# Order of the quarter blocks of two chained MLP products, of their operands and of the last gate mixes, in a one-core decoder layer

## The chip, the cores and the metric

One NeuronCore of one Trainium2 chip runs the whole layer as one program. The metric is device time in microseconds, the median of repeated executions. The kernel before takes 1119.97 us (three runs, 1119.68 to 1120.58).

The core has a matrix engine (TensorE, PE in the profile; its weight loads are PEld), VectorE (DVE), ScalarE (ACT), GpSimd (POOL) and SyncE (SP). In this kernel SP issues the plain loads and POOL issues the DMAs that add what they fetch onto what already lies in SBUF.

## What is computed

One decoder layer on 512 tokens of 1024 features, fp32. Behind the two attention-like branches stand the gated sum, an output projection, and a squared-ReLU MLP of 4096 hidden features:

```python
mixed = jax.nn.sigmoid(gr) * a_ret + jax.nn.sigmoid(gm) * a_mla
x = x + mixed @ w_o

h2 = rms_norm(x, norm_mlp)
x = x + jnp.square(jax.nn.relu(h2 @ w_up)) @ w_down

gate = jax.nn.sigmoid(rms_norm(x, norm_ple) @ w_ple_gate)
x = x + gate * (p_l @ w_ple)
```

The two MLP products and the output projection are what the change touches.

## The kernel before

**Three matmuls for one.** Every fp32 operand is split in two parts that TensorE takes at its fast fp32 rate: ScalarE rounds it (names with h: `wh_`, `ch`, `xu..h`), VectorE subtracts the rounded part from the original (names with l: `wl_`, `cl`, `xu..l`). `mm3` then issues low times high, high times low and high times high. So each weight chunk of 128x1024 costs one ScalarE instruction (line 262) and one VectorE subtraction (line 266) before the matrix engine can use it, in `load_chunk`.

**Seven products for eight.** From the second of four groups on (`gg` = 0 to 3, 1024 hidden features each) the up product (`up_seven`, names `us`, weights `..up<gg><p><c>`) and in all four groups the down product (`down`, names `dn`, weights `..dn<gg><p><c>`) run in seven quarter blocks instead of eight, numbered p = 1 to 7. A block takes its weights in two chunks, c = 0 and 1, of 512 KB. The weights of blocks 1, 2 and 3 are loaded as they are (tiles `wr_`). Block 7 needs a sum of two quarters of the matrix, block 6 that sum with a third quarter added, block 4 with a fourth. These three share one place in SBUF (tile `dr_..7`): a load, an addition by DMA for 7, another for 6 once 7's low part has been taken, another for 4 once 6's has. Block 5 is a sum of two in its own tile. `prepare` (lines 215 to 246) issues the loads on SP (line 234) and the additions on POOL (line 224).

**Operands.** `combine` makes the down product's seven operands from the hidden activations `f` (sums `s`, `s1`, then `xsplit` into `ch`, `cl`). The up product's seven operands `xu1` to `xu7` are made once, in the first group, by `up_operand`, from the normalised input `x2n`, and serve the groups 1 to 3. `down_out` adds a block's result to the output tiles `d` (line 1105).

**What sets the order.** `step` collects the work as a list, and `run_steps` walks it: weights are split one chunk ahead and prepared three chunks ahead. The framework then places each engine's instructions by its own planning, except that matmuls stay in program order. Three buffers each hold the high and the low parts (`NW`), six the raw chunks of blocks 1, 2, 3 and 5 (`NRAW`), four the running sums (`NDRAW`). A high part of a chunk can be written only when TensorE is done with the chunk three before it. Four PSUM tiles of two banks serve the MLP.

Ahead of the MLP, the last part of a branch (`branch_r`, weights `br`) alternates with the gate mixes (`mix`, lines 908 to 912), then come the first halves of two output columns (`out_part`, four of the eight `mixed` operands each), then the rest of the projection (`out_proj`).

The order of the blocks in groups 0 to 2 is one line; a name with u is a block of the next group's up product, a bare number a block of this group's down product:

```python
order = [1, 7, 2, 6, 5, 4, 3]
seq = [1, 7, 2, 6, "u1", 5, "u7", 4, "u6", 3, "u2", "u5", "u4", "u3"]
```

Of the kernel before, what the change touches and what calls it, by code (L numbers as in the profile page):

```python
# [148 lines left out]
def trunk_layer(ctx: ExitStack, tc: tile.TileContext, xT, pT, pos, gains, const, decay, wstream, outT):  # L149
# [52 lines left out]
    offset, o = {}, 0  # L202
# [5 lines left out]
    def step(key, fn, *args):  # L208
        steps.append((key, fn, args))
# [1012 lines left out]
    for h in range(MH):  # L1222
        p, more = h // 2, h + 2 < MH
# [113 lines left out]
            step(None, ret_turned, RH - 1)  # L1337
    for k in range(4):
        step(("br", RH - 1, k), branch_r, RH - 1, k)
        step(None, mix, 2 * k)  # L1340
        step(None, mix, 2 * k + 1)
    for n in range(2):
        step(("o", n), out_part, n, 0)
    for n in range(8):
        step(("o", n), out_proj, n)
    step(None, open_tail)
# [1 line left out]
    for n in range(8):  # L1348
# [9 lines left out]
        elif n in (5, 7):  # L1358
            step(None, up_operand, 1 if n == 5 else 7)

    order = [1, 7, 2, 6, 5, 4, 3]
    seq = [1, 7, 2, 6, "u1", 5, "u7", 4, "u6", 3, "u2", "u5", "u4", "u3"]
    step(None, combine, 0, 1)
    for gg in range(GROUPS):
        last, quarter = gg + 1 == GROUPS, 0
        for p in [1, 7, 2, "e", 6, "e", 5, 4, 3] if last else seq:
            if p == "e":
                if quarter == 0:
                    step(None, ple_in)
                step(("ple", 0), ple, quarter)  # L1370
                quarter += 1
                continue
            if type(p) is str:
                for c in range(2):
                    step(("sw", ("up", gg + 1), int(p[1]), c), up_seven, gg + 1, int(p[1]), c)
                if p == "u5":
                    step(None, combine, gg + 1, 1)
                continue
            if p != 3:
                step(None, combine, gg, order[order.index(p) + 1])  # L1380
            if gg == 0 and p in (1, 7, 2):
                for m in {1: (6,), 7: (2, 5), 2: (4, 3)}[p]:
                    step(None, up_operand, m)
            if last and p == 6:
                step(None, reload_x2)
            for c in range(2):
                step(("sw", ("dn", gg), p, c), down, gg, p, c)
                if last and p == 3 and c == 0:
                    step(None, turn, 0)
                    step(None, turn, 1)  # L1390
            step(None, down_out, gg, p)
    step(("ple", 1), ple, 2)
    step(("ple", 1), ple, 3)
    step(None, turn, 2)
# [59 lines left out]
```

## Time and profile before

| | |
|---|---|
| median of three runs | 1119.97 us |
| the profiled execution's own time | 1120.34 us |
| its span, first to last instruction | 1118.6 us |
| TensorE busy | 1091.0 us, 98% of the span |
| VectorE busy | 757.5 us, 68% |
| ScalarE busy | 565.9 us, 51% |
| granted TensorE clock, mean | 0.997 |
| DMA, mean over the span | 175 GB/s |

How to read it: with TensorE at 98%, time can only come from the places where it stands still or runs at a lower granted clock, so the places matter more than the totals. A matmul's recorded end is modelled, so its last part counts as busy even when nothing follows; the distance between the starts of two blocks tells more than the idle time alone. In the rows below, what stands in brackets is the idle time of that engine just before the instruction and what ended it.

### The profile page before, as it was taken

Reading aid. Unit: us, or ns where it says so; the run is one execution under the profiler, and the core shown is the slowest. Engines: PE = TensorE matmul, PEld = TensorE weight load, DVE = VectorE, ACT = ScalarE, POOL = GpSimd, SP = SyncE. Lnnn points to the kernel's source line nnn. Section 1 sums busy time; section 2 is a strip of 40 time slices with the busy share of each in tenths; the row PEclk is TensorE's granted clock in tenths of the full one; section 3 lists DMA queues with packets and bytes.
Section 4 is the critical chain, followed back from the end, with each engine's and each line's share of the span. In section 5 each row is a group of like instructions: output and inputs, shape, how many; then the busy total and the mean of one; then the engine's idle time right before and its main releaser. Section 6 shows DMA issues by size and latency. Waiting matters only on the chain. (4 is left out here: it accounts for less than half of the span.)

```text
span 1118.6 us, 14885 instructions
## 1 busy us (share of the span) xinstructions
PE 1091.0 (98%) x5569; PEld 924.0 (83%) x5569; DVE 757.5 (68%) x1176; ACT 565.9 (51%) x817; POOL 111.3 (10%) x145
## 2 busy tenths in 40 slices
PE   9999999999999999999999999998999999999998
PEld 7877888888888888888888888886897897888887
DVE  7697677566784655555566486569668678679784
ACT  7637555544466544454554634347454444546551
POOL 0000000001112001121101000001111111111000
PEclk9999999999999999999999999999999999999999
DMA  7242232467788634699846636766888998879511
GB/s 262 64 135 78 64 102 67 132 213 230 179 214 224 206 120 144 167 187 243 190 160 167 212 120 214 232 213 162 202 246 219 216 239 223 205 208 258 178 55 57
DMA packets 64616, 195.91 MB, mean 175 GB/s; under 512 B 7904, under 2 KB 9312, under 8 KB 64160
## 3 DMA queue, kind: packets, MB, share of 16 engines
q1 hardware_dynamic: 46464, 134.90, 35.5%
q0 software_dynamic: 17936, 60.04, 27.6%
q8 instruction: 44, 0.72, 0.3%
q14 instruction: 28, 0.23, 0.1%
q10 hardware_dynamic: 144, 0.03, 0.0%
HBM read 175.80 MB, written 17.04 MB: 172 GB/s over the span
## 5 line engine op out<-in xcount | busy, mean ns | idle before, releaser
L169 PE MATMUL dn<-wl_dn,ch 128*128 128x512 f32 x224 | 89.2, 398 | 9.4 <-DVE wl_dn L266 9.4
L169 PE MATMUL dn<-wh_dn,cl 128*128 128x512 f32 x224 | 88.4, 395 | 2.9 <-ACT wh_dn L262 2.9
L169 PE MATMUL dn<-wh_dn,ch 128*128 128x512 f32 x224 | 87.8, 392 | 0.0
L169 PEld LDWEIGHTS dn<-wl_dn,ch 128*128 128x128 f32 x224 | 42.5, 190 | 21.5 <-DVE wl_dn L266 13.5
L266 DVE TENSOR_TENSOR wl_up<-wr_up,wh_up 128x1024 fp32r<-128x1024 f32 x32 | 39.0, 1222 | 22.1 <-ACT wh_up L262 21.9
L262 ACT ACTIVATE wh_up<-wr_up 128x1024 fp32r<-128x1024 f32 x32 | 33.8, 1055 | 37.7 <-issue 12.7
L169 PEld LDWEIGHTS dn<-wh_dn,cl 128*128 128x128 f32 x224 | 42.4, 189 | 12.5 <-ACT wh_dn L262 3.9
L169 PEld LDWEIGHTS dn<-wh_dn,ch 128*128 128x128 f32 x224 | 42.5, 190 | 8.7
L262 ACT ACTIVATE wh_dn<-wr_dn 128x1024 fp32r<-128x1024 f32 x32 | 33.6, 1056 | 30.2 <-PE us L169 14.6
L262 ACT ACTIVATE wh_rg<-wr_rg 128x1024 fp32r<-128x1024 f32 x28 | 29.6, 1058 | 31.0 <-PE rg L169 12.1
L262 ACT ACTIVATE wh_rv<-wr_rv 128x1024 fp32r<-128x1024 f32 x28 | 29.6, 1058 | 30.4 <-PE rv L169 9.2
L262 ACT ACTIVATE wh_dn<-dr_dn 128x1024 fp32r<-128x1024 f32 x24 | 25.4, 1057 | 34.3 <-PE dn L169 15.3
L266 DVE TENSOR_TENSOR wl_up<-dr_up,wh_up 128x1024 fp32r<-128x1024 f32 x18 | 22.0, 1224 | 30.0 <-ACT wh_up L262 30.0
L266 DVE TENSOR_TENSOR wl_dn<-wr_dn,wh_dn 128x1024 fp32r<-128x1024 f32 x32 | 38.7, 1218 | 3.9 <-ACT wh_dn L262 3.8
L224 POOL DMA_DIRECT2D dr_dn<-wstream x24 | 21.9, 964 | 191.7 <-DVE rx L331 96.8
L266 DVE TENSOR_TENSOR wl_dn<-dr_dn,wh_dn 128x1024 fp32r<-128x1024 f32 x24 | 29.3, 1219 | 16.8 <-ACT wh_dn L262 16.8
L266 DVE TENSOR_TENSOR wl_rg<-wr_rg,wh_rg 128x1024 fp32r<-128x1024 f32 x20 | 24.5, 1226 | 23.6 <-ACT wh_rg L262 23.6
L266 DVE TENSOR_TENSOR wl_rv<-wr_rv,wh_rv 128x1024 fp32r<-128x1024 f32 x20 | 24.4, 1223 | 17.1 <-ACT wh_rv L262 17.1
L262 ACT ACTIVATE wh_up<-dr_up 128x1024 fp32r<-128x1024 f32 x18 | 19.1, 1058 | 28.9 <-DMA dr_up<-wstream 16.2
L266 DVE TENSOR_TENSOR wl_br<-wr_br,wh_br 128x1024 fp32r<-128x1024 f32 x16 | 19.5, 1221 | 19.4 <-ACT wh_br L262 19.4
L1105 DVE TENSOR_TENSOR d<-d,dn 128x1024 f32<-128x1024 f32 x24 | 29.2, 1215 | 3.0 <-PE dn L169 3.0
L262 ACT ACTIVATE wh_br<-wr_br 128x1024 fp32r<-128x1024 f32 x16 | 16.9, 1057 | 21.0 <-issue 12.8
(1889 smaller groups left out, 3684.1 us busy)
## 6 DMA issues: line engine op xcount, KB each, us to landing
wr_up<-wstream SPq DMA_DIRECT2D x32, 512.0 KB, 4.6
wr_dn<-wstream SPq DMA_DIRECT2D x32, 512.0 KB, 6.5
dr_dn<-wstream POOLq DMA_DIRECT2D x24, 512.0 KB, 7.0
wr_rv<-wstream SPq DMA_DIRECT2D x20, 512.0 KB, 4.3
wr_rg<-wstream SPq DMA_DIRECT2D x20, 512.0 KB, 5.2
dr_up<-wstream POOLq DMA_DIRECT2D x18, 512.0 KB, 9.6
wr_rv<-wstream POOLq DMA_DIRECT2D x16, 512.0 KB, 7.4
wr_rg<-wstream POOLq DMA_DIRECT2D x16, 512.0 KB, 6.7
```

The lines of the kernel that those rows point to most:

```text
L169: return tc.keep_in_program_order(nc.tensor.matmul(*a, **k))
L224: nc.gpsimd.dma_start(raw, chunk(("w", blk, kb, fb, c)), accum_op=ALU.add)
L262: i = ACT(hi, raw, AF.Copy, scale=sign)
L266: TT(lo, raw, hi.bitcast(F32), op=ALU.subtract)
L1105: TT(to, to, dps[p], op=ALU.add if sign > 0 else ALU.subtract)
```

## The change

The seven blocks of the down product and the seven of the next group's up product now alternate one by one. Between two blocks whose weights are summed in one place (7, 6, 4) there are always two others. The third block of an up product, which was the last of its group's list, moves behind the first down block of the next group (`v3`). The up product's operands are made one at a time behind five blocks of the first group instead of in three bursts. And the last two mixes move behind the first half of the first output column.

```diff
     for k in range(4):
         step(("br", RH - 1, k), branch_r, RH - 1, k)
+        if k == 3:
+            step(("o", 0), out_part, 0, 0)
         step(None, mix, 2 * k)
         step(None, mix, 2 * k + 1)
-    for n in range(2):
-        step(("o", n), out_part, n, 0)
+    step(("o", 1), out_part, 1, 0)
...
-    seq = [1, 7, 2, 6, "u1", 5, "u7", 4, "u6", 3, "u2", "u5", "u4", "u3"]
+    seq = "1 v3 7 u1 2 6 u7 5 4 u6 3 u2 u5 u4".split()
+    operands = {"2": 6, "5": 2, "4": 5, "3": 4, "u2": 3}
     step(None, combine, 0, 1)
     for gg in range(GROUPS):
         last, quarter = gg + 1 == GROUPS, 0
-        for p in [1, 7, 2, "e", 6, "e", 5, 4, 3] if last else seq:
+        for s_ in "1 v3 7 2 e 6 e 5 4 3".split() if last else seq:
...
+            elif s_[0] in "uv":
+                g_, p = gg + (s_[0] == "u"), int(s_[1])
+                for c in range(2 if g_ else 0):
+                    step(("sw", ("up", g_), p, c), up_seven, g_, p, c)
+                if s_ == "u5":
+                    step(None, combine, g_, 1)
...
-            if gg == 0 and p in (1, 7, 2):
-                for m in {1: (6,), 7: (2, 5), 2: (4, 3)}[p]:
-                    step(None, up_operand, m)
...
+            if gg == 0 and s_ in operands:
+                step(None, up_operand, operands[s_])
```

Three places show what the framework made of it. The first is POOL's queue while group 1 runs: `dr_dn170` and `dr_dn171` are the running sums of down blocks 7, 6 and 4 (chunks 0 and 1), `dr_up27x` those of the next up product, `wr_..15x` and `wr_..25x` the sums of the blocks 5. Before:

```order
L224 DMA wr_dn150_7853<-wstream 128x1024
L224 DMA wr_dn151_7873<-wstream 128x1024
L224 DMA dr_dn170_7668<-wstream 128x1024
L224 DMA dr_dn171_7707<-wstream 128x1024
L224 DMA dr_dn170_7668<-wstream 128x1024
L224 DMA dr_dn171_7707<-wstream 128x1024
L224 DMA wr_up250_8160<-wstream 128x1024
L224 DMA wr_up251_8180<-wstream 128x1024
L224 DMA dr_up270_7905<-wstream 128x1024
L224 DMA dr_up271_7943<-wstream 128x1024
```

And in the changed program, from the same place on:

```order
L224 DMA wr_dn150_7919<-wstream 128x1024
L224 DMA wr_dn151_7939<-wstream 128x1024
L224 DMA dr_dn170_7663<-wstream 128x1024
L224 DMA dr_dn171_7683<-wstream 128x1024
L224 DMA dr_dn170_7663<-wstream 128x1024
L224 DMA dr_dn171_7683<-wstream 128x1024
L224 DMA dr_up270_7874<-wstream 128x1024
L224 DMA dr_up271_7900<-wstream 128x1024
L224 DMA wr_up250_8160<-wstream 128x1024
L224 DMA wr_up251_8180<-wstream 128x1024
```

The additions for down block 6 still stand behind those for block 5; those for up block 6 now stand ahead of those for up block 5.

The second place is VectorE at the start of group 0, between the low parts of the first and the second down block (`wl_dn011`, `wl_dn070`, `wl_dn071`). Of the changed program:

```order
L308 TENSOR_TENSOR xu6l0_7119<-x2n0_6698,xu6h_7118 128x512
L266 TENSOR_TENSOR wl_dn011_6928<-wr_dn011_6849,wh_dn011_6927 128x1024
L308 TENSOR_TENSOR xu2l0_7273<-x2n1_6768,xu2h0_7271 128x512
L308 TENSOR_TENSOR xu2l1_7274<-x2n1_6768,xu2h1_7272 128x512
L308 TENSOR_TENSOR xu5l0_7322<-x2n0_6698,xu5h0_7320 128x512
L308 TENSOR_TENSOR xu5l1_7323<-x2n0_6698,xu5h1_7321 128x512
L313 SCALAR_TENSOR_TENSOR xu4l0_7429<-x2n1_6768,xu4h0_7427 128x512
L984 SCALAR_TENSOR_TENSOR f01_6835<-up06_6851,bcx2_6692 128x512 x2
L266 TENSOR_TENSOR wl_dn070_6948<-dr_dn070_6880,wh_dn070_6947 128x1024
L308 TENSOR_TENSOR xu6l1_7120<-x2n0_6698,xu6h_7118 128x512
L1070 TENSOR_TENSOR s_0_6921<-f01_6835,s_0_6921 128x1024
L266 TENSOR_TENSOR wl_dn071_6973<-dr_dn071_6931,wh_dn071_6972 128x1024
```

The operands of blocks 6, 2, 5 and 4 stand ahead of `wl_dn070` as they did before, now with one more instruction among them (`xu4l0`, which stood behind `wl_dn071`); `cl02`, which stood ahead of `wl_dn071`, now stands behind it. Behind these rows come `cl02`, `s1_0` and then `wl_up110`, the first weights of the up block that now follows; before, `wl_up110` came only after the four down blocks.

The third place is VectorE at the start of the last group, up to the low part `cl32` of the operand of down block 2. Of the changed program:

```order
L1067 TENSOR_TENSOR s_3_9098<-f30_8576 128x1024
L266 TENSOR_TENSOR wl_up331_9144<-wr_up331_9108,wh_up331_9143 128x1024
L1105 TENSOR_TENSOR d0_6965<-d0_6965,dn31_9110 128x2x512
L308 TENSOR_TENSOR cl37_9101<-s_3_9098,ch37_9100 128x1024
L266 TENSOR_TENSOR wl_dn370_9175<-dr_dn370_9127,wh_dn370_9174 128x1024
L1070 TENSOR_TENSOR s_3_9098<-f31_8577,s_3_9098 128x1024
L266 TENSOR_TENSOR wl_dn371_9211<-dr_dn371_9147,wh_dn371_9210 128x1024
L1044 TENSOR_SCALAR f31_8577<-us31_8522 128x4x256
L266 TENSOR_TENSOR wl_dn320_9230<-wr_dn320_9178,wh_dn320_9229 128x1024
L308 TENSOR_TENSOR ppl_9292<-praw_9289,pph_9291 128x1024
L266 TENSOR_TENSOR wl_dn321_9254<-wr_dn321_9214,wh_dn321_9253 128x1024
L308 TENSOR_TENSOR cl32_9207<-f31_8577,ch32_9206 128x1024
```

Before, `f31` (line 1044) came right behind the first down block's weights and `cl32` right behind `s_3` of line 1070; now `f31` waits for the moved up block, and five rows stand between that sum and `cl32`.

More of the change, by code (lines that the diff above doesn't have):

```diff
@@ L1365, in trunk_layer @@
         last, quarter = gg + 1 == GROUPS, 0
-        for p in [1, 7, 2, "e", 6, "e", 5, 4, 3] if last else seq:
-            if p == "e":
+        for s_ in "1 v3 7 2 e 6 e 5 4 3".split() if last else seq:
+            if s_ == "e":
                 if quarter == 0:
@@ L1371, in trunk_layer @@
                 quarter += 1
-                continue
-            if type(p) is str:
-                for c in range(2):
[L1375 to L1380, printed above, removed]
-            if gg == 0 and p in (1, 7, 2):
-                for m in {1: (6,), 7: (2, 5), 2: (4, 3)}[p]:
-                    step(None, up_operand, m)
[L1384 to L1391, printed above, removed]
+            elif s_[0] in "uv":
[4 more added lines that the diff above has]
+                    step(None, combine, g_, 1)
+            else:
+                p = int(s_)
+                if p != 3:
+                    step(None, combine, gg, order[order.index(p) + 1])
+                if last and p == 6:
+                    step(None, reload_x2)
+                for c in range(2):
+                    step(("sw", ("dn", gg), p, c), down, gg, p, c)
+                    if last and p == 3 and c == 0:
+                        step(None, turn, 0)
+                        step(None, turn, 1)
+                step(None, down_out, gg, p)
+            if gg == 0 and s_ in operands:
+                step(None, up_operand, operands[s_])
     step(("ple", 1), ple, 2)
```

## The prediction

> **What bounds the kernel now.** I read the page's busy times first.
>
> ```profile
> PE 1091.0 (98%) x5569; PEld 924.0 (83%) x5569; DVE 757.5 (68%) x1176; ACT 565.9 (51%) x817; POOL 111.3 (10%) x145
> ```
>
> TensorE is busy for 98% of the span, and the change removes no matmul. So it can win only what TensorE loses in waits and in clock. The list of waits, one row for each kind (engine and tile, releaser: sum, count, longest), says what it waits for in the stages touched.
>
> ```profile
> PE dn L169 <- DVE wl_dn L266: 9.4, 9, 2.8
> PE us L169 <- DVE wl_up L266: 4.1, 5, 1.2
> ...
> PE dn L169 <- ACT wh_dn L262: 2.9, 2, 1.5
> ```
>
> These make 16.4 us of idle time, all of it weights of the MLP that come late. A matmul's end is modelled, so the loss is better read from lengths. The windows below run from the first down block of a group to that of the next, and the last from there to the end of its down blocks (length, busy us of PE, PEld, DVE, ACT and POOL with counts, granted clock, DMA share, GB/s).
>
> ```profile
> 756.99:846.03 89.04, 82.12 (x506) 72.49 (x504) 65.65 (x63) 49.40 (x54) 13.96 (x16) 0.98 0.83 208
> 846.03:930.55 84.52, 79.87 (x507) 71.66 (x505) 61.87 (x54) 39.99 (x40) 13.93 (x16) 1.00 0.91 225
> 930.55:1015.31 84.76, 79.86 (x507) 71.66 (x505) 61.88 (x54) 39.99 (x40) 13.12 (x15) 1.00 0.81 210
> 1015.31:1060.65 45.34, 45.34 (x211) 37.67 (x209) 39.55 (x36) 26.79 (x28) 4.35 (x5) 1.00 0.80 228
> ```
>
> VectorE has 62 us of work in 84.5, so it is not the bound. What makes a weight late is in the chain that ended last, here in group 1 (start, length, what).
>
> ```profile
> 846.38 4.35 DMA wr_dn<-wstream
> ...
> 851.84 0.55 POOL dr_dn L224
> 852.38 13.93 DMA dr_dn<-wstream
> ...
> 866.42 1.07 ACT wh_dn L262
> ...
> 867.51 1.24 DVE wl_dn L266
> ...
> 871.58 5.75 PE us L169 x48
> 877.33 5.48 PE dn L169 x24
> ```
>
> An undisturbed up block takes 5.75 us and a down block 5.48. The addition for down block 6 (chunk 1) leaves POOL at 852.38, lands at 866.31, and reaches TensorE through ScalarE and VectorE at 868.79.
>
> **The change part by part: groups 1 and 2.** Seven blocks of each kind without loss make 7 × (5.75 + 5.48) = 78.6 us. Against this group 1 loses 84.52 − 78.6 = 5.9 and group 2 84.76 − 78.6 = 6.2. Does the new order remove it all? I count from T, the end of block 4 of group 1's up product, where VectorE takes its result:
>
> ```profile
> 840.47 1.22 DVE L1047 TENSOR_TENSOR f<-f,us 128x1024 f32<-128x1024 f32 x1 [0.51 <-PE us L169]
> ```
>
> In before, up block 3 (5.75) and down blocks 1, 7 and 2 (16.4) follow, so chunk 1 of down block 6 is due a chunk (2.7) later, at T + 24.9; it was ready at 868.79, T + 28.3, so 3.5 late. Now block 1, up 3, block 7, up 1 and block 2 stand ahead, 3 × 5.48 + 2 × 5.75 = 27.9, and chunk 1 is due at T + 30.7. POOL's rows show the block 5 additions still ahead of these two. What releases them is block 7's low parts, which VectorE takes in the order as before; so I let them leave at the same T + 11.9, land at T + 25.8 and be ready at T + 28.3. That is 2.3 us in hand, and the wait is gone. Up block 6 likewise gets two blocks in front (5 and 4 instead of 4 alone, 5.5 us more) for the 2.5 us it loses now. The moved up block 3 takes all it issues with it: two loads on SP, two roundings, two subtractions, its 48 matmuls and the result on lines 1044 and 1045. Its place used to cover the first operand sums of the group (lines 1048, 1067 and `cl`): they are needed for down block 7, which now has down 1 and up 3 in front, so the cover stays. What is late next is VectorE's queue, about 1.14 us per 128x1024 instruction, which I count two to three us ahead of TensorE throughout. The alternation changes the kind of block more often. No row shows a price; between 0 and 0.1 us for each I take nothing, as 871.58 + 5.75 = 877.33 shows one passing free. **Groups 1 and 2: −12.1.**
>
> **Group 0** loses most at its start. Up to the end of its fourth down block:
>
> ```profile
> 756.99:788.85 31.86, 25.16 (x97) 18.62 (x96) 29.09 (x32) 20.97 (x26) 5.21 (x6) 0.95 0.70 154
> 785.00:787.00 2.00, 2.00 (x7) 1.54 (x6) 2.00 (x3) 0.00 (x0) 0.86 (x1) 0.54 0.49 33
> 787.00:789.00 2.00, 2.00 (x8) 1.60 (x7) 2.00 (x2) 0.00 (x0) 0.00 (x0) 0.61 0.71 147
> ```
>
> Four blocks take 31.86 instead of 21.9, so 9.9 are lost, in waits and in a low clock behind the last. TensorE's timeline has the waits (the bracket is the idle time just before), VectorE's what stands ahead of the weights:
>
> ```profile
> 765.57 0.50 PE L169 MATMUL dn<-wl_dn,ch 128*128 128x512 f32 x1 [1.74 <-DVE wl_dn L266]
> 784.63 0.50 PE L169 MATMUL dn<-wl_dn,ch 128*128 128x512 f32 x1 [2.82 <-DVE wl_dn L266]
> ```
>
> ```profile
> 759.56 1.22 DVE L266 TENSOR_TENSOR wl_dn<-wr_dn,wh_dn 128x1024 fp32r<-128x1024 f32 x1 [0.43 <-ACT wh_dn L262]
> 760.70 1.28 DVE L308 TENSOR_TENSOR xu2l<-x2n,xu2h 128x512 fp32r<-128x512 f32 x2
> 761.90 1.29 DVE L308 TENSOR_TENSOR xu5l<-x2n,xu5h 128x512 fp32r<-128x512 f32 x2
> ...
> 764.31 1.21 DVE L266 TENSOR_TENSOR wl_dn<-dr_dn,wh_dn 128x1024 fp32r<-128x1024 f32 x1
> ...
> 767.18 1.22 DVE L308 TENSOR_TENSOR cl<-f,ch 128x1024 fp32r<-128x1024 f32 x1
> 768.32 1.21 DVE L266 TENSOR_TENSOR wl_dn<-dr_dn,wh_dn 128x1024 fp32r<-128x1024 f32 x1
> ```
>
> The diff spreads the operands, but VectorE's order hardly does: those of blocks 6, 2 and 5 still stand ahead of `wl_dn070`, and one of block 4's (0.60, half of the 1.20 from 760.70 to 761.90) joins them. With the 0.43 us wait gone, `wl_dn070` moves by +0.17, to 764.48, so the wait at block 7 grows from 1.74 to 1.74 + 0.17 + 0.43 = 2.3 us (the chunk ahead of it starts 0.43 earlier). `wl_dn071` moves by +0.60 − 0.43 − 1.14 (`cl02` now behind it) to 767.35 and no longer delays. Behind it come `cl02`, `s1_0` and `wl_up110`, at 1.14 each: ready at 772.0, while TensorE, which starts block 7's second chunk at 768.6, would be free 2.7 us later, at 771.3, so up block 1 starts at 772.0 after a wait of 0.7. From there nothing is late: the additions for block 6 have up 1 and down 2 in front. Up 1, down 2 and down 6 end at 772.0 + 5.75 + 2 × 5.48 = 788.7; before, the four down blocks alone ended at 788.85, and with up 1 the same work at 794.6. **−5.9**, and 0.5 more at up block 6, since the other ten blocks, 89.04 − 31.86 = 57.18, would take 3 × 5.48 + 7 × 5.75 = 56.7: **−6.4**. The 2.82 us gap and the low clock behind it are in this sum. In these terms only the places where work lies are estimates: a microsecond more on VectorE ahead of `wl_dn070` is paid in full, one less is won.
>
> **The projection.** The second half of the mixed operands used to stand ahead of `wl_o` for the second column:
>
> ```profile
> 665.51 0.68 DVE L308 TENSOR_TENSOR mix4l<-re,mix4h 128x512 fp32r<-128x512 f32 x1
> ...
> 669.12 1.22 DVE L266 TENSOR_TENSOR wl_o<-wr_o,wh_o 128x1024 fp32r<-128x1024 f32 x1
> ```
>
> ```profile
> 670.39 0.50 PE L169 MATMUL wo<-mix0h,wl_o 128*128 128x512 f32 x1 [0.56 <-DVE wl_o L266]
> ```
>
> In the changed program's order `wl_o` comes right behind `mix4l`, ready near 667.3, and TensorE wants it at about 669.7. The wait (0.6 idle, 0.7 from start to start, slower first matmuls) goes: **−0.8**. The mixes behind have slack, since the first full column part starts only after this one.
>
> **The last group** had no idle time (45.34 busy of 45.34). Now `cl32`, the operand of down block 2, stands fourteen instructions behind line 1047's addition, that group's T. At 1.14 each (767.18 to 768.32 above), with 0.3 for `wl_dn321`, whose buffer comes free only with down 7's first chunk, it starts at T + 16.3 and is done at 17.5. Block 2 is due after down 1, up 3 and down 7, 5.48 + 5.75 + 5.48 = 16.7. A new wait, bounded by 0 and, with one instruction more in between, 2: I take **+0.8**.
>
> **Sum:** −12.1 − 6.4 − 0.8 + 0.8 = −18.5. The profiled execution took 1120.34 us (1118.6 of span and 1.7 around it), so 1101.8; the median was 0.37 lower, so **1101.5**.
>
> **The rivals.** *The clock drops again in group 0.* Before, a gap of 2.82 us was followed by 4 us at 0.54 and 0.61, one of 1.74 was not; the 2.3 us that stay lie between. Price: 2 × 0.46 + 2 × 0.39 = 1.7, so 1103.2; chance 0.15. [...]
>
> *The additions land later.* Their flight is not fixed:
>
> ```profile
> dr_dn<-wstream POOLq DMA_DIRECT2D x24, 512.0 KB, 7.0
> ```
>
> The median is 7.0 us, and the one above took 13.93 with loads beside it; DMA is at 0.91 in group 1, and a denser group moves the same bytes in 78.6 us. With 4 us later, the 2.3 in hand leave 1.7 late at down 6 in groups 1 and 2 and about as much at the two up blocks 6: 3 to 6 us back, 1104.5 to 1107.5; chance 0.17. [...]
>
> *The other side: POOL's queue.* Down 6's additions stand behind those of block 5, which wait for a raw load (the 4.35 us piece of the chain) and that for a free buffer. If this comes more than 2.3 us later relative to T, each further us is paid in three groups. To eat 18.5 + 2.2 us takes 9 us later, a landing at T + 35: then above 1122, slower. Against it: the raw chunks are used up in an order that is hardly slower than before. With other new waits of the kind: chance 0.05.
>
> *The operands do get out of the way.* If the waits of group 0 vanish too (2.3 + 0.7, the 0.2 between them, and 0.8 of the last group), 1097.5; chance 0.07. VectorE's order speaks against it.
>
> **How the numbers follow.** The forecast as above has 0.56. The range reaches over the rivals but the slower one, from 1097.5 to 1107.5. A measurement of this kernel can tell about 0.2%, 2.2 us, from no change. Faster by more: 0.92; within it: 0.03; slower: 0.05, all from the queue rival and its milder part.
>
> **What would show it.** In the changed profile the distance from one down block 1 to the next should be 78.6 us in groups 1 and 2, with no wait of TensorE on `wl_dn` or `wl_up` there; in group 0 one wait of about 2.3 us at block 7 and 0.7 at up 1, the clock at 1.00 behind them; no wait at `wo`; some 0.8 us on `cl` in the last group; and the additions for down 6 landing near T + 26. An addition that lands after T + 28 in group 1, or a clock below 0.9 in group 0, would make the forecast wrong; so would VectorE, if its queue shows no idle time ahead of late weights.

## The result, and the profile after

The changed kernel takes **1101.99 us** (median of four runs, 1101.0 to 1106.24) where the kernel before takes 1119.84 (four runs, 1119.68 to 1120.58): a ratio of 0.9847, 95% interval 0.9821 to 0.9873, 17.9 us less. The forecast was 1101.5, with a range of 1097.5 to 1107.5. The profiled execution took 1101.0 us with a span of 1099.2, against 1120.34 and 1118.6.

The page's busy times after:

```profile
PE 1085.2 (99%) x5569; PEld 923.3 (84%) x5569; DVE 757.9 (69%) x1176; ACT 565.8 (51%) x817; POOL 111.1 (10%) x145
```

The matmuls and every other engine have the same work as before. TensorE counts as busy for 5.8 us less with the same matmuls; the mean granted clock rose from 0.997 to 0.999, and a 128x512 matmul right behind a wait is counted longer (0.50 us in the rows below, 0.39 otherwise). The same windows as before, from the first down block of a group to that of the next (up block 3 has moved from the end of one window to the start of the next, so the first is an up block shorter, the last one longer):

```profile
755.63:832.07 76.44, 73.78 (x458) 65.76 (x456) 59.58 (x57) 46.49 (x51) 13.89 (x16) 1.00 0.88 223
832.07:910.57 78.50, 78.50 (x507) 71.83 (x505) 62.10 (x53) 40.04 (x39) 13.92 (x16) 1.00 0.93 240
910.57:989.07 78.50, 78.50 (x507) 71.84 (x505) 61.92 (x53) 40.04 (x39) 12.19 (x14) 1.00 0.89 229
989.07:1041.33 52.26, 51.38 (x258) 43.42 (x257) 45.23 (x40) 29.73 (x30) 5.21 (x6) 1.00 0.77 223
```

In groups 1 and 2 TensorE is busy for the whole of 78.50 us: no wait is left. The chain that ended last says the same for group 1. Where it ran through POOL, a DMA, ScalarE and VectorE before, it is TensorE's blocks alone:

```profile
843.45 5.47 PE dn L169 x24
848.92 5.75 PE us L169 x48
854.67 10.91 PE dn L169 x48
```

The addition for down block 6 that was late before is now in time. POOL issues the two of group 1 here, and VectorE takes the low part of the second one, ready at 859.78, while TensorE comes to that chunk at 862.70:

```profile
843.36 2.09 POOL L224 DMA_DIRECT2D dr_dn<-wstream  x2
```

```profile
858.55 1.23 DVE L266 TENSOR_TENSOR wl_dn<-dr_dn,wh_dn 128x1024 fp32r<-128x1024 f32 x1 [0.61 <-ACT wh_dn L262]
```

What is left of the MLP's waits stands at the start of group 0 and in the last group. TensorE's timeline, rows with an idle time ahead of them, from down block 7 to up block 1 and at down block 2 of the last group:

```profile
761.87 0.51 PE L169 MATMUL dn<-wh_dn,cl 128*128 128x512 f32 x1 [0.54 <-ACT wh_dn L262]
763.88 0.50 PE L169 MATMUL dn<-wl_dn,ch 128*128 128x512 f32 x1 [1.50 <-DVE wl_dn L266]
770.16 0.39 PE L169 MATMUL us<-xu1h,wl_up 128*128 128x256 f32 x1 [0.62 <-DVE wl_up L266]
```

```profile
1006.79 0.50 PE L169 MATMUL dn<-wh_dn,cl 128*128 128x512 f32 x1 [0.87 <-DVE cl L308]
```

VectorE's timeline shows why block 7 still waits: the diff spread the operands, its queue did not.

```profile
757.27 1.22 DVE L266 TENSOR_TENSOR wl_dn<-wr_dn,wh_dn 128x1024 fp32r<-128x1024 f32 x1
758.40 1.28 DVE L308 TENSOR_TENSOR xu2l<-x2n,xu2h 128x512 fp32r<-128x512 f32 x2
759.61 1.28 DVE L308 TENSOR_TENSOR xu5l<-x2n,xu5h 128x512 fp32r<-128x512 f32 x2
760.81 0.68 DVE L313 SCALAR_TENSOR_TENSOR xu4l<-x2n,xu4h 128x512 fp32r<-128x512 f32 x1
761.42 1.28 DVE L984 SCALAR_TENSOR_TENSOR f<-up,bcx 128x512 f32<-128x512 f32 x2
762.62 1.21 DVE L266 TENSOR_TENSOR wl_dn<-dr_dn,wh_dn 128x1024 fp32r<-128x1024 f32 x1
```

Between the low part for down block 1 and that for block 7 stand five half-size instructions for operands, 758.40 to 761.42, whose results TensorE first uses at 814.80.

### The profile page after: what moved, and what is told of

It reads as the page before. It is cut to its first block, busy times and chain, and to the rows that moved or that the text cites. A ratio compares the mean times of both kernels' runs of the same rounds, so it can differ in the third digit from the quotient of the medians.

```text
span 1099.2 us, 14887 instructions
## 1 busy us (share of the span) xinstructions
PE 1085.2 (99%) x5569; PEld 923.3 (84%) x5569; DVE 757.9 (69%) x1176; ACT 565.8 (51%) x817; POOL 111.1 (10%) x145
## 5 line engine op out<-in xcount | busy, mean ns | idle before, releaser
L262 ACT ACTIVATE wh_up<-wr_up 128x1024 fp32r<-128x1024 f32 x32 | 33.9, 1058 | 44.1 <-PE us L169 13.4
L169 PEld LDWEIGHTS dn<-wh_dn,cl 128*128 128x128 f32 x224 | 42.1, 188 | 10.5 <-DVE cl L308 1.3
L169 PEld LDWEIGHTS dn<-wl_dn,ch 128*128 128x128 f32 x224 | 42.1, 188 | 10.3 <-DVE wl_dn L266 2.3
L266 DVE TENSOR_TENSOR wl_dn<-wr_dn,wh_dn 128x1024 fp32r<-128x1024 f32 x32 | 39.0, 1220 | 10.7 <-ACT wh_dn L262 10.6
L262 ACT ACTIVATE wh_rg<-wr_rg 128x1024 fp32r<-128x1024 f32 x28 | 29.6, 1059 | 30.4 <-PE rg L169 12.1
L266 DVE TENSOR_TENSOR wl_dn<-dr_dn,wh_dn 128x1024 fp32r<-128x1024 f32 x24 | 29.3, 1220 | 13.9 <-ACT wh_dn L262 13.9
L262 ACT ACTIVATE wh_up<-dr_up 128x1024 fp32r<-128x1024 f32 x18 | 19.1, 1062 | 25.9 <-PE dn L169 14.1
L873 ACT ACTIVATE rt<-br 128x512 f32<-128x512 f32 x24 | 13.9, 594 | 25.8 <-PE br L169 25.8
```

The costliest lines, as they stand in the source:

```text
L169: return tc.keep_in_program_order(nc.tensor.matmul(*a, **k))
L262: i = ACT(hi, raw, AF.Copy, scale=sign)
L266: TT(lo, raw, hi.bitcast(F32), op=ALU.subtract)
L873: ACT(t, ps, AF.Copy)
```

## The experiments

Twelve runs follow, on three chips; each is compared with runs of the kernel before on its own chip. Medians in us, lowest and highest in brackets, ratio to the kernel before with its 95% interval:

| run | what differs | time | ratio |
|---|---|---|---|
| e1_order_only | before, with the new order alone | 1103.43 (1102.34 to 1103.52) | 0.9844 [0.9816, 0.9873] |
| e2_mix_only | before, with the mixes moved | 1118.76 (1116.41 to 1123.55) | 0.9993 [0.9971, 1.0015] |
| e3_operands_only | before, with the operands spread | 1122.51 (1118.61 to 1124.62) | 1.0016 [0.9998, 1.0035] |
| e4_six_sooner | changed, one block between 7 and 6 | 1112.79 (1110.05 to 1115.52) | 0.9924 [0.9896, 0.9952] |
| e8_control | changed, again | 1102.21 (1101.5 to 1103.17) | 0.9833 [0.9811, 0.9856] |
| e5_three_back | changed, up block 3 at its old place | 1100.75 (1099.93 to 1101.04) | 0.9817 [0.9795, 0.9839] |
| e6_ple_between | changed, a ple quarter ahead of down 2 | 1101.59 (1101.07 to 1102.3) | 0.9828 [0.9805, 0.985] |
| e7_pinned | changed, group 0's operands forced late | 1103.61 (1102.25 to 1104.31) | 0.9844 [0.9821, 0.9866] |
| e20_three_back_again | e5 once more | 1101.05 (1100.6 to 1101.59) | 0.9827 [0.9804, 0.9851] |
| e12_first_pinned | e5, operands kept behind the weights of the first four blocks only | 1100.04 (1097.41 to 1100.87) | 0.9814 [0.9789, 0.9839] |
| e19_seven_ahead | e5, three blocks between 7 and 6 | 1110.39 (1110.11 to 1111.98) | 0.9913 [0.9893, 0.9932] |
| e18_pinned_seven_ahead | e12 and e19 together | 1109.32 (1107.43 to 1110.24) | 0.9898 [0.9876, 0.992] |

### The three parts apart

**e1_order_only** takes the new `seq`, the last group's new list and nothing else:

```diff
-    seq = [1, 7, 2, 6, "u1", 5, "u7", 4, "u6", 3, "u2", "u5", "u4", "u3"]
+    seq = "1 v3 7 u1 2 6 u7 5 4 u6 3 u2 u5 u4".split()
```

> The new order of the blocks with the moved third block, but the operands in their three old bursts and the mixes at their old place. Theory (the order carries nearly everything, the parts add up): the changed kernel's time plus 1.4 us for the lost mixes (the difference that the two traces show up to the first down block) plus about 1 us at the first up block of group 0, where the old bursts put about two more half-size instructions ahead of its weights: 1104 to 1105. Rival (the spread operands are what lets the order work): group 0 keeps its old waits, 1107 or more.

1103.43: the order alone wins 15.7 us beside its own runs of before (1119.13). That is 0.6 us below the expected range. Of the three kinds of wait on the MLP's weights that stood in the list of before, one is left in its own, all of it at the start of group 0; in groups 1 and 2 there is none. A wait of the size expected at up block 1 stands a chunk earlier, at the second chunk of block 7 (0.97 us), and the one on the operand in the last group is longer than in the changed kernel (1.48 for 0.87).

```profile
PE dn L169 <- DVE wl_dn L266: 3.3, 3, 1.7
```

**e2_mix_only** moves `out_part` for the first column ahead of the last two mixes.

> The kernel before with only the last two mixes moved. As forecast the wait ahead of the second output column goes, -0.8 us: 1119.1. If the wait at the seventh chunk of the first up product goes with it, as in the changed kernel's trace, -1.4 us: 1118.5. Rival (the gain is taken up by a later wait): no change, 1119.9.

The times cannot tell it from no change (the interval holds 1). The traces can: in e2's the second column's part follows the first without a wait; e1, with the mixes at their old place, still has it in TensorE's timeline:

```profile
670.57 0.50 PE L169 MATMUL wo<-mix0h,wl_o 128*128 128x512 f32 x1 [0.55 <-DVE wl_o L266]
```

The other 0.7 us, at the sixth and seventh chunk of the first up product, are not the mixes' doing: that wait is there in e2's trace and gone in e1's. It goes with the reload of `x2n` from memory ahead of it: VectorE stands idle before line 994 for 4.1 us in the kernel before and in e2, for 2.9 and 3.3 in the changed kernel and in e1. As far as the profiles show, this goes with the program and not with the execution: both profiled executions of the changed kernel (the second is e8's) are without the wait, and both of e5's kernel have it (0.5 and 0.9 us from start to start). Why the reload lands earlier in some orders is not shown.

**e3_operands_only** gives the kernel before the dictionary `operands` in place of its three bursts.

> The kernel before with only the operands made one at a time, at the same blocks as in the changed kernel. Theory: VectorE's order hardly changes and down block 6 of group 0 waits for its additions anyway, so what comes earlier ahead of block 7's second chunk (1 us) is waited for again at block 6: 1119 to 1120. Rival (the bursts were the cause of group 0's waits): -3 us or more, 1117 or less.

No measurable gain, and the median lies above the expectation. Its list of waits, against that of before, shows the waits on down weights (`wl_dn`) smaller, 5.4 for 9.4 us, and those on up weights larger, 9.8 for 4.1:

```profile
PE us L169 <- DVE wl_up L266: 9.8, 5, 3.8
PE dn L169 <- DVE wl_dn L266: 5.4, 9, 1.5
PE dn L169 <- ACT wh_dn L262: 1.9, 2, 1.3
```

In group 0 the waits ahead of up block 1 fall from 6.7 to 3.2 us, and those at up block 6 rise from 0.2 to 4.7, where the chain runs through an addition of 14.3 us. So what goes at the start of group 0 is waited for again at a later addition, though at up block 6 and not at down block 6 as expected. The parts are not equal partners: the order carries nearly everything.

### Is it the distance between two sums?

**e4_six_sooner** keeps the alternation and the moved block and takes one block out from between 7 and 6:

```diff
-    seq = "1 v3 7 u1 2 6 u7 5 4 u6 3 u2 u5 u4".split()
+    seq = "1 v3 7 2 6 u1 u7 5 4 u6 3 u2 u5 u4".split()
```

> The changed kernel, but up block 1 behind down block 6 instead of ahead of it, in the groups 0 to 2: only down block 2 stands between down 7 and down 6, all else still alternates. Theory (what counts is the time between 7 and 6): in the changed trace the second addition lands 25.3 us after the last up block's end and is ready at 27.7; it would now be due at 24.9, so 2.8 us are lost in groups 1 and 2 each, and 1 to 2.5 in group 0: 1108 to 1110. Rival (the alternation or the moved third block as such wins the time, by an even load of the queues): 1102 to 1104.

1112.79, 10.6 us above the control's 1102.21 (on another chip) and 2.8 above the expected range: the rival falls, the size was too small. In the profiled execution, the slowest of the six, group 1 takes 84.49 us again, not 78.50, and the chain that ended last runs as it did before the change, through POOL and the addition:

```profile
835.72:920.21 84.49, 81.26 (x506) 72.84 (x505) 61.99 (x54) 39.91 (x39) 13.90 (x16) 0.98 0.91 225
```

```profile
847.99 14.64 DMA dr_dn<-wstream
...
862.71 1.06 ACT wh_dn L262
...
865.08 4.05 PE dn L169 x11
```

The 6.0 us lost in this group are 1.0 at down block 2, whose operand is late without up block 1 ahead of it (as in the last group; this I had left out), some 4.4 at the two chunks of down 6, and 0.4 behind them. Part of this is the clock, which stood at 0.59 and 0.56 from 866 to 870, behind the wait. Group 2, at a clock of 1.00, takes 83.35 and so loses 4.9. That group 1 comes out at the length of before is a coincidence: there some 3.5 us went at down 6 and 2.5 at up 6, and up 6 does not wait here. The addition took 14.64 us to land here, 13.2 in the changed kernel (issued at 844.1, landed at 857.3).

### Up block 3 need not move

**e8_control** is the changed kernel again, as a mark.

> The changed kernel once more, as the mark for the next three on this chip: 1101 to 1104. If one run of it is 3 us or more above the others again, as one of the four so far (1106.24 at a mean clock of 0.996), then something in it varies; the first theory is the clock behind the gap at down block 7 of group 0 (2 us of idle time).

No run of it stood out; 1106.24 stays a single one without a trace. But its profile shows something else: the clock behind the gap at down block 7. The two windows, first of the changed kernel's profile, then of the control's (the eighth figure is the clock):

```profile
764.00:766.00 2.00, 2.00 (x9) 1.66 (x10) 2.00 (x3) 2.00 (x3) 1.49 (x2) 1.00 0.00 0
766.00:768.00 2.00, 2.00 (x9) 1.44 (x9) 2.00 (x3) 2.00 (x3) 1.13 (x2) 1.00 0.86 141
```

```profile
764.00:766.00 2.00, 2.00 (x7) 1.59 (x7) 2.00 (x3) 2.00 (x3) 1.68 (x2) 0.66 0.28 18
766.00:768.00 2.00, 2.00 (x6) 1.51 (x6) 2.00 (x3) 2.00 (x3) 0.93 (x2) 0.50 0.83 131
```

The same gap of 2.04 us (0.54 and 1.50 around one matmul in the one, 0.53 and 1.51 in the other), and a clock of 1.00 in one execution, 0.66 and 0.50 in another. From the start of down 1 to that of up 1 it is 14.53 us in the one and 15.22 in the other. The drop costs 0.7 us between these two executions and not the 1.7 of slow matmuls; the wait at up block 1 is gone in return.

**e5_three_back** puts the third up block back at the end of its group's list:

```diff
-    seq = "1 v3 7 u1 2 6 u7 5 4 u6 3 u2 u5 u4".split()
+    seq = "1 7 u1 2 6 u7 5 4 u6 3 u2 u5 u4 u3".split()
...
-        for s_ in "1 v3 7 2 e 6 e 5 4 3".split() if last else seq:
+        for s_ in "1 7 2 e 6 e 5 4 3".split() if last else seq:
```

> The changed kernel with the third up block back at the end of its group's list and the last group's list without it, the alternation otherwise the same. Theory (two blocks between 7 and 6 do the work, the moved third block only makes down block 2's operand late in the last group): 1.0 us below the control, and no wait on the operand in the last group. Rival (the moved block is needed, because block 7's weights or operand are late without it behind block 1): 1 us or more above the control, with waits in groups 1 and 2.

1100.75, 1.5 us below the control, and no run of the one overlaps with one of the other (1099.93 to 1101.04, 1101.5 to 1103.17). In the last group it is 2.95 us from the second chunk of block 7 to block 2, where the control has 3.76; groups 1 and 2 are as full as with the moved block, 78.48 us each. So the move wins nothing there and costs about 1 us in the last group, by the wait that it makes. The traces do not give the 1.5 us of the medians: e5's has 0.4 us more at block 1 of group 0 and 0.5 more at the reload of `x2n`, and the two profiled executions differ by 0.5.

**e6_ple_between** tries to cover the same wait by one quarter of the ple product.

> The changed kernel with one quarter of the ple product moved ahead of down block 2 in the last group. Theory: the quarter's 2.72 us cover the operand that is 1.0 us late; 1.0 us below the control. Rival (VectorE is the bound there, and the quarter's own weights come ahead of the operand): the same as the control, the wait only moves.

0.6 us below the control, with overlapping runs, and the trace agrees with the rival: the operand is in time, but TensorE now waits 0.95 us for the weights of down block 6, which stand in VectorE's queue behind operands of the later blocks.

```profile
1010.46 1.23 DVE L1076 TENSOR_TENSOR s<-f,f 128x1024 f32<-128x1024 f32 x1
1011.59 1.23 DVE L1070 TENSOR_TENSOR s<-f,s 128x1024 f32<-128x1024 f32 x1
1012.81 1.23 DVE L308 TENSOR_TENSOR cl<-s,ch 128x1024 fp32r<-128x1024 f32 x1
1013.95 1.22 DVE L266 TENSOR_TENSOR wl_dn<-dr_dn,wh_dn 128x1024 fp32r<-128x1024 f32 x1
```

### What hides behind the wait in group 0

**e7_pinned** keeps the roundings of five operands and of all weights of group 0's down and group 1's up blocks in the list's order on ScalarE:

```diff
-        if key[0] == "a1":
+        if key[0] == "a1" or (key[0] == "sw" and key[1] in (("dn", 0), ("up", 1))):
             tc.keep_in_program_order(i)
...
-            split(src[:, 2 * c:2 * c + 2], None, scale, hi=hi, lo=lo)
+            split(src[:, 2 * c:2 * c + 2], None, scale, hi=hi, lo=lo, pin=p not in (1, 7))
```

> The changed kernel with the roundings of the five operands and of the weights of group 0's down blocks and group 1's up blocks kept in the order of the list on ScalarE, so that the operands' work really leaves the place ahead of down block 7. Theory (VectorE's queue, the operands in it, is what keeps block 7 and up block 1 waiting): the four chunks at the start of group 0 lose 3.7 us in the changed kernel's trace (3.52 + 4.63 + 3.66 + 2.97 against 3 x 2.72 + 2.88); nearly all of it goes, 3 to 3.7 us below the control. Rival (the wait is for the additions of block 7 or for a weight buffer): the same as the control, or up to 1 us below. If the clock behind the gap is what varies, the spread of this kernel's runs is smaller than the control's.

1.4 us *above* the control, so the expected size is missed by 4.4 us and more. The wait at block 7 is gone, as the theory said, but others stand in its place: TensorE's timeline has these, at up block 1, down block 6 and up block 7,

```profile
770.08 0.38 PE L169 MATMUL us<-xu1h,wl_up 128*128 128x256 f32 x1 [0.45 <-DVE wl_up L266]
782.64 0.50 PE L169 MATMUL dn<-wl_dn,ch 128*128 128x512 f32 x1 [0.76 <-DVE wl_dn L266]
786.13 0.36 PE L169 MATMUL us<-xu7h,wl_up 128*128 128x256 f32 x1 [0.71 <-DVE wl_up L266]
```

and the chain that ended last has one more, at up block 2, where the fixed order keeps a weight behind an operand and that behind a result (`d`) that waits for TensorE:

```profile
814.94 0.03 ACT d L1105
...
815.86 1.14 ACT xu4h L312 x2
817.01 0.95 ACT wh_up L262
```

Its runs spread over 2.1 us and the control's over 1.7, so the smaller spread that was expected if the clock is what varies is not there, although its profile has neither the gap at block 7 nor a drop of the clock.

**e12_first_pinned** starts from e5 and holds only the weights of down blocks 1, 7 and 2 and up block 1 ahead of the operands; `operands` becomes `{"2": 6, "6": 2, "u7": 5, "5": 4, "u2": 3}`. **e20_three_back_again** is its mark.

> The three-back version, and on ScalarE the roundings of the five operands kept behind those of the weights of group 0's down blocks 1, 7 and 2 and of up block 1 only; the later weights are free again, and the operand of up block 4 comes two blocks earlier than in the pinned run. Theory (the wait at block 7 hid the additions for down 6 of group 0, which leave only once the block 5 additions have left, so that they become the bound when it goes; the other losses of the pinned run came from weights held behind operands on ScalarE): no wait up to up block 1, about 2 us at down block 6, no 1.6 us wait at up block 2; 0.5 to 1.5 us below the mark. Rival (the operands' work costs the same wherever it stands, since VectorE has no room in group 0): the same as the mark or above.

> The version with the third up block back at its old place (the fastest so far) once more, as the mark for the next three: 1100 to 1101.5.

1100.04 against 1101.05, as expected in size, though the runs overlap (1097.41 to 1100.87, 1100.6 to 1101.59). The windows from the start of group 0's down block 1 to that of block 5, first of the mark, then of e12, then of the changed kernel, which has the same blocks there:

```profile
756.42:794.48 38.06, 35.78 (x194) 30.55 (x193) 35.23 (x37) 27.93 (x33) 6.92 (x8) 0.96 0.83 193
```

```profile
756.09:793.08 36.99, 34.75 (x194) 29.28 (x193) 30.80 (x31) 23.80 (x26) 6.95 (x8) 1.00 0.83 184
```

```profile
755.63:792.67 37.04, 34.38 (x194) 29.21 (x192) 34.58 (x36) 27.95 (x33) 6.94 (x8) 1.00 0.83 192
```

The pins (the roundings held in order) win 1.1 us over the mark, whose profile has the clock drop behind the gap at block 7 (and at block 1 takes 0.4 us more than the changed kernel), but nothing over the changed kernel's profile, which has the gap and no drop. So the waits only move. Those at block 7 are gone, and so is e7's at up block 2; 0.45 us of idle time are left at up block 1, and down block 6 takes 2.6 us too long. How much of the 1.0 us between the medians is the clock that no longer falls is not shown; the mean clocks of the runs, 0.999 to 1.0 with the pins and 0.998 without, fit it.

The additions for down 6 are the bound now, as the chain shows: POOL issues them only once the second addition for block 5 has left (766.13), which had waited for its load.

```profile
758.80 6.75 DMA wr_dn<-wstream
...
766.13 0.52 POOL wr_dn L224
...
767.43 13.85 DMA dr_dn<-wstream
```

VectorE had taken the low parts that they replace by 761.1 and 764.6, so POOL's queue held them for 2.8 us and more. But the second one left no later than in the mark (767.43, there 768.21) and flew longer, 13.85 us for 9.46, with SP's next load beside it 4.5 us earlier. No run separates the two.

**e19_seven_ahead** and **e18_pinned_seven_ahead** give these additions one block more, without the pins and with them:

```diff
-    seq = "1 7 u1 2 6 u7 5 4 u6 3 u2 u5 u4 u3".split()
+    seq = "1 7 u1 2 u7 6 5 u6 4 3 u2 u5 u4 u3".split()
```

> The three-back version with up block 7 ahead of down block 6, so that three blocks stand between down 7 and down 6, still two between the others of the sums; nothing pinned. Theory (two blocks were enough, nothing waits for additions any more): the same as the mark within 0.5 us. Rival (additions land so unevenly that more distance pays): 1 us or more below.

> Both edits together. Theory: with three blocks between, the additions for down 6 of group 0 are due 5.7 us later, and their wait goes as well as the one at block 7: 2.5 to 3.5 us below the mark, 1097 to 1098.5. Rival (VectorE has no room in group 0): the same as the pinned run beside it.

Both miss: 1110.39 is 9.3 us above the mark, and 1109.32 is 9.3 above e12 and 10.8 above the expected range. The list of waits of e19 names a releaser that is in the list of neither kernel, `d` on line 1105, which takes a finished block out of PSUM:

```profile
PE us L169 <- DVE d L1105: 4.1, 3, 1.5
PE dn L169 <- DVE d L1105: 2.8, 2, 1.4
PE dn L169 <- DVE wl_dn L266: 1.8, 2, 1.5
```

Group 1's rows are these, up block 7 right behind down 2 and down 5 right behind down 6:

```profile
864.63 0.39 PE L169 MATMUL us<-xu7h,wl_up 128*128 128x256 f32 x1 [1.31 <-DVE d L1105]
877.51 0.47 PE L169 MATMUL dn<-wh_dn,cl 128*128 128x512 f32 x1 [1.41 <-DVE d L1105]
```

In the program, down blocks 6 and 5 go through one PSUM tile (that of block 1, `onto`), so 5 cannot start before 6 has been taken out (in group 0 by ScalarE, on line 1103); and up block 7 opens a fifth tile where there are four, while those of down 1, 7 and up 1 are still in use, so it waits for down 2's. From start to start it is 1.3 to 1.6 us at each of these places, two in each of three groups, which is the 9 us. The change's order keeps off both, as the order before did, which I had not seen in it: an order has to separate not only the sums but the users of a PSUM tile. In e18 no wait for the additions for down 6 is left, so the third block does what it was put in for, but the PSUM waits cost more.

## Why the prediction was right

**Groups 1 and 2** were the largest term, −12.1. The windows went from 84.52 and 84.76 to 78.50 each, −12.3; the forecast length was 78.6. The mechanism holds in its own numbers. T, VectorE's row behind up block 4, is 832.27 in group 1 of the changed kernel; the second addition for down 6 left at T + 11.9 (forecast T + 11.9), landed at T + 25.1 (forecast 25.8) and was ready at T + 27.5 (forecast 28.3), so 2.9 us were in hand at block 6 (forecast 2.3). In group 2 it landed at T + 26.4 and 1.7 were in hand. e4 shows the price of one block less in the same place.

**Group 0**, forecast −6.4, came to 89.04 − 76.44 − 5.75 = −6.85. The waits that I left standing stood: 2.04 us at block 7 for 2.3, 0.62 at up block 1 for 0.7, and for the reason given, the operands ahead of the weights on VectorE.

**The projection**, −0.8: the wait is gone. By the starts its two parts now follow at 2.72 us where they took 3.44, −0.7.

**The last group**, +0.8: the operand of down block 2 is late by 1.0 (3.76 us from the second chunk of block 7 to block 2, for 2.72). The window came to 52.26 − 45.34 − 5.75 = 1.2 us more than before.

**The sum** was −18.5. By these four it is −18.7, and no term is off by more than half a microsecond, so no error stands hidden behind another. The two profiled executions differ by 19.3, of which 0.7 is the wait on the reload of `x2n`, which the forecast did not have; the medians differ by 17.9.

**Rivals.** *The clock drop* does happen behind a 2 us gap, in some executions (the last section counts them), and that the profiled one had none was chance: its chance was set as if the gap's length decided, and its price of 1.7 was too high, 0.7 by the control. Nor does a clock below 0.9 in group 0 make the forecast wrong, as the prediction said it would: the control's profile has one, at 1101.5 us. *Later additions* did come, but not where it mattered. The median flight of the additions into `dr_dn` rose from 7.0 to 9.5 us, and in group 1 those for up block 4 and for the next group's down block 7 took 10.6 to 15.3 us (5.5 to 10.5 before), landing 6 us and more before TensorE came to them. The second addition for down 6 took 13.2 us in group 1 and 14.3 in group 2, about as before (13.9 and 14.1). *POOL's queue* did not make them late in the changed kernel, but it is a part of what limits e12. *The operands out of the way* was priced at 1097.5 as if their waits were the last ones; e7 and e12 show a second bound close behind, the additions for down 6. Of the 3.7 us lost at group 0's start in the changed kernel's profile, e12 has nothing back by the start of block 5 (36.99 us for 37.04). What the prediction took for a part of the mechanism and is none is the moved up block: it wins nothing that e5 does not have, and costs its 1 us in the last group.

**Open.** The run at 1106.24 has no trace; that the clock explains it is not shown. No run puts the additions for block 6 ahead of those for 5 in POOL's queue. The best version run is e12_first_pinned, 0.9814 [0.9789, 0.9839] of the kernel before; that it beats the changed kernel rests on e5's gain; the 1.0 us beyond that lie within overlapping runs, and the traces tie them to the clock at least in part.

## What to carry to other kernels

Where weights are built up in place by DMAs, add up flight, rounding and subtraction (13.2 + 1.1 + 1.2 = 15.5 us in group 1 here, from the issue on, a microsecond more in group 2) and let the order put a little more matmul time than that between two users: with two blocks between 7 and 6 it is 16.7 us from chunk to chunk, with one about 11. With two, no wait for these sums is left in groups 1 and 2; what a third would win by itself isn't shown, since it ran into PSUM. Before an order is changed further, list everything that its neighbours share, PSUM tiles as well as sums: one swap that was free for the weights cost 9 us in PSUM. And a wait that is priced as removable should be priced against the wait that stands behind it: in e3, e6, e7 and e12 one went and another took its place.

## What the runs showed of the hardware

After the same gap of 2.04 us on TensorE the granted clock stayed at 1.00 in the changed kernel's profile and fell to 0.66 and 0.50 in the control's (means of 2 us). Eight profiled executions have a gap of 2.02 to 2.07 us at this place: the clock fell behind it in four (e5, e8, e19, e20, each with a mean of 0.998 over its execution) and in the other four not (the changed kernel, e4 and e6, at 1.00 from 766 to 768, and e3, whose matmuls behind it start 0.23 us apart). So at this length it is not the gap alone that decides; in the kernel before, one of 1.74 us was not followed by a drop and one of 2.82 was. What else decides is not shown. In the control the clock stood at 0.50 for 3.41 us, from 764.65 to 768.06; in the kernel before, behind the gap of 2.82, for 3.41 us as well, from 785.16 to 788.57.

An addition by DMA of 512 KB took between 5.3 and 15.3 us from issue to landing in the changed kernel's trace; those of 13 us and more were all issued within 1.3 us behind another. In e7, where SP's next two loads left 3.9 and 2.3 us earlier, the two for down 6 of group 0 took 10.3 and 13.4 us, in the changed kernel 8.5 and 9.9. No run changed the loads alone, so that loads lengthen additions is not shown.

A 128x512 matmul on the split parts takes TensorE 0.23 us from start to start (24 of them in the 5.48 of a down block). What the same product would take on unsplit operands no run shows.
